# Sixteen gate columns of a gated DeltaNet: out of a product of their own, into a 272-wide group of the value projection

## The chip, the cores and the metric

The kernel runs on one core of a Trainium2 chip. The time is device microseconds for one execution of the whole program, and the figure given for a version is the median of its runs. Before the change the median is 1522.89 us of three runs (1521.16 to 1525.27).

In the listings PE is TensorE (matmuls and transposes; PEld is its weight load), ACT is ScalarE, DVE is VectorE, POOL is GpSimd, and SP is SyncE, which issues most DMAs. A tile is a buffer in the core's memory, with 128 partitions; a bank is one of the eight accumulator banks that PE writes.

## The reference, cut to what matters

The program computes one layer of a diffusion backbone: 1024 latent tokens and 256 context tokens of width 1024, together 1280 tokens, ten tiles of 128. What the change touches is the combined input projection and the gates made from 16 of its columns:

```python
h = concatenate([modulate(rms_norm(ctx)), modulate(rms_norm(x))])
p = h @ w_in
qkv_a, z, ab, rq, rk, rv, rg = split(p)      # 1536, 512, 16, 512, 512, 512, 512 columns
q, k, v = short_conv(qkv_a)                  # gated DeltaNet
a_f, a_b, b_f, b_b = split(ab, 4)            # 4 heads x 2 directions x 2 gates
g_f = -exp(A[0]) * softplus(a_f + dtb[0])    # g_b alike from a_b
o = gated_delta_rule(q, k, v, g_f, sigmoid(b_f))   # both directions
# retention on rq, rk, rv, then gates, output projection, SwiGLU, final RMSNorm
```

## The kernel before, in words

Everything is fp32. A large product is made of three matmuls: the operands are split into a high part (`hhi`, `whi`) and a remainder (`hlo`, `wlo`), and high times high, high times low and low times high are summed. `hhi` and `hlo` hold the normalized, modulated tokens with channels on partitions: 8 slices of 128 channels by 1280 tokens.

The stages that matter follow each other in the text like this.

- **Modulation** (L241 to L275). Tokens come in groups: two of 256 tokens, then one of 512 and one of 256 context tokens. Each tile is scaled on DVE (L259), transposed on PE (L266, tile `xtr`), and modulated. For the two later groups ACT writes `hhi` (L241) straight from the bank, DVE writes the scaled copy `hf` (L243), and DVE or POOL the remainder `hlo` (L244).
- **Value columns of retention** (`rv`), groups g = 0 and 1 of 256 columns each, by `token_major` (L334 to L350). The weights are loaded in two halves (`wraw`), split by ACT (`whi`, L287) and DVE (`wlo`, L288). For each of ten token tiles 24 matmuls (L343 to L345) fill a bank `tm` taken from the three `pa` banks, with a slice of `hhi` or `hlo` as the stationary 128x128 operand and 256 weight columns as the moving one. `fin_copy` on ACT copies the bank to `res` (L365), and a DMA that ACT issues stores it (L350). The latent tiles come first, the context tiles last. A bank can be filled again only when what was in it has been read.
- **The rest of adaLN** (`ada_rest`, L293): DVE sums (`acc`), then two short matmuls with a column of ones (`gr`, L309).
- **The gate columns** (L404 to L422). The 16 columns' weights `wabr` are loaded and split into 32 stationary columns (high and low beside each other). In three chunks of 256, 512 and 512 tokens, 48 matmuls `ab` (L413, L414) make a product with channels on partitions (32 x 1280). ACT copies it (L415), PE transposes it back in ten pieces (`abT`, L418), DVE copies and adds high and low (L420, L422). The result, `xa`, has tokens on partitions. What follows (softplus, `beta`, cumulative sums `G`, L423 to L456) reads `xa`.
- **The convolution blocks** (`conv_block`, L459 to L481): 12 blocks of 128 channels, channel-major, matmuls of 256 or 512 tokens (L468 to L470), two ACT evacuations, four taps on DVE, a SiLU on ACT. For keys and queries `kstat` (L488) transposes the result (`kt`). Between them stand `ada_rest` and more `token_major` groups (`rg` among them, from pool W2).
- **The solve** (`pre`, L557 to L600): for each token tile the product `kk` on PE (L557), decay matrices `e` on POOL (L575, L577), their product `ut` on DVE (L587), and then a triangular inverse that begins with a memset of `X` on POOL (L612).

The program is not issued in the order of the text. It is built with `schedule_with_timeline_sim=True`: a scheduler with a model of the engines orders each engine's instructions once, at build time. Each engine then works off its own row in that order, and waits at the head of the row where an operand isn't there yet or a buffer isn't free.

Of the kernel before, what the change touches and what calls it, by code (L numbers as in the profile page):

```python
# [8 lines left out]
F32 = mybir.dt.float32  # L9
F32R = mybir.dt.float32r  # L10
I32 = mybir.dt.int32
AF = mybir.ActivationFunctionType
ALU = mybir.AluOpType
# [4 lines left out]
P = 128  # L18
D = 1024
KT = D // P  # L20
NCTX = 256
NLAT = 1024
NTOK = NCTX + NLAT
TT = NTOK // P
# [13 lines left out]
def build(nc, tc, ap, dbg=None, stop=None, marks=None):  # L38
    root = ExitStack()
    V, S, G, T, SY = nc.vector, nc.scalar, nc.gpsimd, nc.tensor, nc.sync  # L40

    def pool(name, bufs=1, side=None, space=None):
        kw = {}
        if side is not None:
            kw["side"] = side
        if space is not None:
            kw["space"] = space
        if space is not DRAM:
            kw["reuse_waits"] = "tile"
        es = ExitStack()  # L50
        p = es.enter_context(tc.tile_pool(name=name, bufs=bufs, **kw))
        root.push(es)
        p_close[id(p)] = es
        return p
# [31 lines left out]
    def bank(tag, name):  # L86
        return PS["pool"].tile([P, 512], F32, tag=tag, name=name, bufs=PS["tags"][tag])

    def bank_a(name):
        return bank("pa", name)  # L90

    def bank_b(name):
        return bank("pb", name)
# [6 lines left out]
    def const(name, shape):  # L100
        t = C.tile(shape, F32, tag=name, name=name)
        S.dma_start(t, ap[name])
        return t
# [14 lines left out]
    def rsqrt_mean(pl, q, n, tag, num, x=None):  # L118


        s = pl.tile([P, n], F32, tag=tag + "s", name=tag + "s")
        y = pl.tile([P, n], F32, tag=tag + "y", name=tag + "y")
        u = pl.tile([P, n], F32, tag=tag + "u", name=tag + "u")
        if x is None:
            S.activation(s, q, AF.Sqrt, bias=epsb, scale=1.0 / num)
            x = pl.tile([P, n], F32, tag=tag + "x", name=tag + "x")
            V.tensor_scalar(x, q, -0.5 / num, -0.5 * EPS, ALU.mult, ALU.add)
            half = 1.0
        else:
            S.activation(s, x, AF.Sqrt)  # L130
            half = -0.5
        V.reciprocal(y, s)
        if n == 1 and half == 1.0:
            V.tensor_scalar(u, y, y, x, ALU.mult, ALU.mult)
        else:
            V.scalar_tensor_tensor(u, y, half, x, ALU.mult, ALU.mult)
            V.tensor_tensor(u, u, y, ALU.mult)
        V.scalar_tensor_tensor(y, u, 1.5, y, ALU.add, ALU.mult)
        return y
# [21 lines left out]
    try:  # L161

        cc = const("cc", [P, KT, 2])
        ident = const("ident", [P, P])
# [8 lines left out]
        hhi = LH.tile([P, KT, NTOK], F32R, tag="hhi", name="hhi")  # L173
        hlo = LH.tile([P, KT, NTOK], F32R, tag="hlo", name="hlo")
        W = pool("w", bufs=2)
# [18 lines left out]
        for k in range(KT):  # L194
            for i in range(2):
                w = P0.tile([P, 1024], F32, tag="adaw", name="adaw", bufs=7)
                last_ada = SY.dma_start(w, ap["ada_w"][k * P:(k + 1) * P, i * 1024:(i + 1) * 1024]).ins
                kw = {"skip_group_check": True} if k else {}
                if 2 * k + i in PLAIN:

                    for j in range(2):
                        T.matmul(psr[2 * i + j][:2, :], csl[:, k, :], w[:, j * 512:(j + 1) * 512],
                                 start=False, stop=(k == KT - 1), **kw)
                    continue
                whi = P0.tile([P, 1024], F32R, tag="adahi", name="adahi", bufs=2)
                wlo = P0.tile([P, 1024], F32R, tag="adalo", name="adalo", bufs=2)
                S.activation(whi, w, AF.Copy)
                V.tensor_tensor(wlo, w, whi.bitcast(F32), ALU.subtract)
                for j in range(2):
                    js = slice(j * 512, (j + 1) * 512)  # L210
                    o = psr[2 * i + j][:4, :]
# [8 lines left out]
        for i in range(2):  # L220
# [3 lines left out]
            for j in range(8):  # L224
                c0 = 4 * (8 * i + j)
# [20 lines left out]
        for gi, grp in enumerate(XGROUPS):  # L246
            n, t0 = len(grp), grp[0]
# [32 lines left out]
        R2 = pool("r2", bufs=2)  # L280
# [5 lines left out]
        def split(raw, hi, lo, e):  # L286
            S.activation(hi, raw, AF.Copy)  # L287
            e.tensor_tensor(lo, raw, hi.bitcast(F32), ALU.subtract)  # L288
# [30 lines left out]
                if c == 4:  # L319
                    V.scalar_tensor_tensor(o, o, 1.0, gffn[:, ks], ALU.add, ALU.mult)  # L320

        def weights(src, shape, e, pl, q=S, after=None):
            raw = pl.tile([P] + shape, F32, tag="wraw", name="wraw")
            if after is None:
                q.dma_start(raw, src)
            else:
                with tc.issue_after(after):
                    q.dma_start(raw, src)
            hi = pl.tile([P] + shape, F32R, tag="whi", name="whi")
            lo = pl.tile([P] + shape, F32R, tag="wlo", name="wlo")  # L330
            split(raw, hi, lo, e)
            return hi, lo

        def token_major(g, tiles, finish, store, pl, q=S, after=None):  # L334

            w = [weights(ap["wt"][g, :, 4 * kh:4 * kh + 4, :], [4, 256], V, pl, q, after) for kh in range(2)]
            c0 = (g % 2) * 256
            for t in tiles:
                tsl = slice(t * P, (t + 1) * P)
                o = bank_a("tm")[:, 0:256]  # L340
                for k in range(KT):
                    whi, wlo = w[k // 4]
                    T.matmul(o, hhi[:, k, tsl], whi[:, k % 4, :], start=(k == 0), stop=False)  # L343
                    T.matmul(o, hhi[:, k, tsl], wlo[:, k % 4, :], start=False, stop=False)  # L344
                    T.matmul(o, hlo[:, k, tsl], whi[:, k % 4, :], start=False, stop=(k == KT - 1))  # L345
                res = R1.tile([P, 256], F32, tag="res", name="res")
                finish(t, o, res)
                nm = GROUPS[g // 2]
                dst = zd[t - 2, :, c0:c0 + 256] if nm == "z" else rd[t, :, RD[nm], c0:c0 + 256]
                store.dma_start(dst, res)  # L350
# [20 lines left out]
        for g in range(2):  # L371
            token_major(g, ALL, fin_copy, S, W, SY, last_ada)
            ada_rest(2, g)
# [21 lines left out]
        AB = pool("ab", side="right")  # L395
# [4 lines left out]
        tri = AB.tile([P, 2, P], F32, tag="tri", name="tri")  # L400
        SY.dma_start(tri, ap["tri"])
        CHUNKS = [(0, 256), (256, 512), (768, 512)]

        wabr = AB.tile([P, KT, 16], F32, tag="wabr", name="wabr")  # L404
        SY.dma_start(wabr, ap["wab"])
        wab = AB.tile([P, KT, 32], F32R, tag="wab", name="wab")
        split(wabr, wab[:, :, 0:16], wab[:, :, 16:32], V)

        abc = AB.tile([32, NTOK], F32, tag="abc", name="abc")
        for c0, n in CHUNKS:  # L410
            ps = bank_b("ab")
            for k in range(KT):
                T.matmul(ps[:32, :n], wab[:, k, :], hhi[:, k, c0:c0 + n], start=(k == 0), stop=False)  # L413
                T.matmul(ps[:32, :n], wab[:, k, :], hlo[:, k, c0:c0 + n], start=False, stop=(k == KT - 1))  # L414
            S.activation(abc[:, c0:c0 + n], ps[:32, :n], AF.Copy)  # L415
        ps = bank_b("abT")
        for t in range(TT):
            T.transpose(ps[:, t * 32:(t + 1) * 32], abc[:, t * P:(t + 1) * P], ident[:32, :32])  # L418
        abT = AB.tile([P, TT, 32], F32, tag="abT", name="abT")
        V.tensor_copy(abT.rearrange("p t c -> p (t c)"), ps[:, :TT * 32])  # L420
        xa = AB.tile([P, TT, 16], F32, tag="xa", name="xa")
        V.tensor_tensor(xa, abT[:, :, 0:16], abT[:, :, 16:32], ALU.add)  # L422
        av = AB.tile([P, TT * 8], F32, tag="av", name="av")  # L423
        V.tensor_tensor(av.rearrange("p (t c) -> p t c", c=8), xa[:, :, 0:8],
                        bc(small["dtb"], [P, TT, 8], 1), ALU.add)
# [10 lines left out]
        ps = bank_b("G")  # L436
# [14 lines left out]
        ps = bank_b("GT")  # L451
# [86 lines left out]
        for g in (6, 7):  # L538
            token_major(g, LAT, fin_gate, S, W2, SY)
# [163 lines left out]
        for h in range(H):  # L703
            y = newy()
            conv_block(8 + h, y, False)
            for t0, n in ((0, 2), (2, 4), (6, 4)):
                ps = bank_b("vT")
# [22 lines left out]
        for g in (8, 9):  # L730
            token_major(g, LAT, fin_gate, S, W)
# [546 lines left out]
        w = {}  # L1278
# [52 lines left out]
        def finish(i, h):  # L1331
            l = 4 * h + i
            ssx = FO.tile([P, 1], F32, tag="ssx", name="ssx", bufs=4)
            V.tensor_tensor(ssx, sq[l][:, 0:1], sq[l][:, 1:2], ALU.add)
            rs = rsqrt_mean(FO, ssx, 1, "r%d" % i, D)
            G.tensor_tensor(xo[l][:, 0], xo[l][:, 0], fgr[:, 0], ALU.mult)
            for n in range(2):
                if n == 0:
                    S.activation(xo[l][:, 0], xo[l][:, 0], AF.Copy, scale=rs)
                else:  # L1340
                    V.scalar_tensor_tensor(xo[l][:, n], xo[l][:, n], rs, fgr[:, n], ALU.mult, ALU.mult)
                SY.dma_start(ap["out"][l * P:(l + 1) * P, n * 512:(n + 1) * 512], xo[l][:, n])
# [134 lines left out]
```

## Time and profile before

| | |
|---|---|
| median of three runs | 1522.89 us (1521.16 to 1525.27) |
| the profiled execution | 1518.69 us, its span 1516.9 us |
| mean granted TensorE clock | 0.977 |
| DVE / ACT / POOL busy, share of the span | 65% / 40% / 42% |
| modulation of the last two groups, with first matmuls of `rv` | about 50 to 80 us |
| matmuls of `rv`, `rk` and others, then `ab` | 80 to 125.4 us |
| convolution blocks and token-major groups | about 126 to 286.6 us |
| first `kk` that the solve waits for | 286.76 us |

Times in the listings are microseconds from the start of the span unless marked ns. In a group's row "x704" is the number of instructions. In a timeline row the first number is the start, the second the duration, and brackets at the end show idle time ahead of the instruction and what ended it. PE runs its matmuls overlapped, so the distance from one start to the next, not the duration of one, says what a matmul costs.

### The profile page before, as it was taken

The numbers are of one execution on the slowest core, as the hardware profiler recorded it, in microseconds if no ns is written. First come the engines' busy times: TensorE is split into PE (matmuls) and PEld (weight loads), VectorE is DVE, ScalarE is ACT, GpSimd is POOL, SyncE is SP. The second block draws the span as 40 slices with busy tenths as digits, with TensorE's granted clock in tenths as the row PEclk, the third lists the DMA queues.
The fourth block names the chain that finished last, engine by engine and source line by source line (L and its number), as shares of the span: only waits on it lengthen the run. The fifth ranks groups of instructions, "written<-read, shape, count | busy, mean of one in ns | idle before, by whom it ended". The sixth has DMA issues, their size and how long they took to land.

```text
span 1516.9 us, 24335 instructions
## 1 busy us (share of the span) xinstructions
PE 1441.7 (95%) x8973; PEld 1241.0 (82%) x8973; DVE 986.2 (65%) x1943; ACT 612.6 (40%) x1268; POOL 637.2 (42%) x589
## 2 busy tenths in 40 slices
PE   7899999987999999999689899999999999999997
PEld 1798887976989899999568778887888888888886
DVE  4955689379776634678847787655655555557477
ACT  4733454456451111325534443233333333354444
POOL 0300001476123233324306669889755553235321
PEclk9899999999989999999999999999999999999999
DMA  9374576587586464996843336676322232685962
GB/s 362 101 236 138 165 228 213 164 256 238 167 240 183 141 210 166 344 407 210 279 126 130 139 139 216 223 245 226 137 105 104 105 105 90 216 301 189 308 200 111
DMA packets 156487, 298.15 MB, mean 197 GB/s; under 512 B 43385, under 2 KB 75465, under 8 KB 150993
## 3 DMA queue, kind: packets, MB, share of 16 engines
q1 hardware_dynamic: 116624, 246.88, 48.3%
q10 hardware_dynamic: 36944, 41.08, 8.6%
q0 software_dynamic: 2800, 8.65, 1.6%
q8 instruction: 70, 1.15, 0.3%
q14 instruction: 49, 0.39, 0.1%
HBM read 206.60 MB, written 89.96 MB: 196 GB/s over the span
## 4 chain that ended last, share of the span: by engine, by line
PE 56%; POOL 8%; DVE 8%; DMA 7%; issue 4%; ACT 3%; ACTq 0%; SPq 0%; POOLq 0%; DVEq 0%
PE ffn L1168 6%; PE ffn L1166 6%; PE ffn L1167 6%; PE fo L1292 5%; PE fo L1294 5%; PE fo L1293 5%; PE tm L344 3%; PE tm L345 3%; PE tm L343 3%; DMA wd<-tw 2%; PE op L1026 1%; PE op L1027 1%; PE op L1025 1%; DMA gw<-grow_d 1%; POOL ws L1139 1%
## 5 line engine op out<-in xcount | busy, mean ns | idle before, releaser
L344 PE MATMUL tm<-wlo,hhi 128*128 128x256 f32 x704 | 205.3, 293 | 5.6 <-DVE wlo L288 5.6
L343 PE MATMUL tm<-whi,hhi 128*128 128x256 f32 x704 | 203.7, 293 | 5.9 <-ACT whi L287 2.4
L345 PE MATMUL tm<-whi,hlo 128*128 128x256 f32 x704 | 204.0, 292 | 0.0
L344 PEld LDWEIGHTS tm<-wlo,hhi 128*128 128x128 f32 x704 | 139.1, 198 | 8.4 <-DVE wlo L288 6.7
L343 PEld LDWEIGHTS tm<-whi,hhi 128*128 128x128 f32 x704 | 138.1, 198 | 8.0 <-ACT whi L287 3.0
L345 PEld LDWEIGHTS tm<-whi,hlo 128*128 128x128 f32 x704 | 138.6, 197 | 0.5 <-POOL hlo L244 0.2
L1166 PE MATMUL ffn<-t,whi 128*128 128x512 f32 x352 | 136.8, 390 | 1.4 <-ACT whi L287 1.4
L1168 PE MATMUL ffn<-t,wlo 128*128 128x512 f32 x352 | 136.9, 390 | 0.8 <-DVE wlo L288 0.8
L1167 PE MATMUL ffn<-t,whi 128*128 128x512 f32 x352 | 137.0, 389 | 0.0
L287 ACT ACTIVATE whi<-ws 128x512 fp32r<-128x512 f32 x88 | 55.6, 632 | 173.6 <-PE ffn L1167 122.3
L288 DVE TENSOR_TENSOR wlo<-ws,whi 128x512 fp32r<-128x512 f32 x88 | 95.1, 1082 | 46.9 <-ACT whi L287 46.7
L287 ACT ACTIVATE whi<-wraw 128x512 fp32r<-128x512 f32 (+1 forms) x98 | 75.2, 771 | 124.4 <-PE ffn L1167 81.6
L1293 PE MATMUL fo<-wlo,ahi 128*128 128x512 f32 x308 | 119.8, 389 | 0.0
L1292 PE MATMUL fo<-whi,ahi 128*128 128x512 f32 x308 | 119.3, 389 | 0.0
L1294 PE MATMUL fo<-whi,alo 128*128 128x512 f32 x308 | 119.0, 389 | 0.0
L288 DVE TENSOR_TENSOR wlo<-wraw,whi 128x512 fp32r<-128x512 f32 (+1 forms) x92 | 98.7, 1075 | 18.1 <-ACT whi L287 18.1
L1166 PE MATMUL ffn<-b,whi 128*128 128x512 f32 x264 | 103.9, 393 | 3.9 <-ACT whi L287 3.9
L1168 PE MATMUL ffn<-b,wlo 128*128 128x512 f32 x264 | 103.9, 393 | 2.1 <-DVE wlo L288 2.1
L1167 PE MATMUL ffn<-b,whi 128*128 128x512 f32 x264 | 103.4, 392 | 0.0
L468 PE MATMUL b<-hhi,whi 128*128 128x512 f32 (+1 forms) x256 | 94.2, 368 | 0.3 <-ACT y L472 0.3
L469 PE MATMUL b<-hlo,whi 128*128 128x512 f32 (+1 forms) x256 | 94.2, 368 | 0.0
L470 PE MATMUL b<-hhi,wlo 128*128 128x512 f32 (+1 forms) x256 | 93.9, 367 | 0.0
(431 smaller groups left out, 3586.4 us busy)
## 6 DMA issues: line engine op xcount, KB each, us to landing
adaw<-ada_w SPq DMA_DIRECT2D x48, 512.0 KB, 5.1
pk<-sd SPq DMA_DIRECT2D x16, 1536.0 KB, 7.9
wraw<-wfi SPq DMA_DIRECT2D x44, 512.0 KB, 3.7
ar<-ad SPq DMA_DIRECT2D x33, 512.0 KB, 4.6
w<-wfo SPq DMA_DIRECT2D x22, 512.0 KB, 5.1
wd<-tw SPq DMA_DIRECT2D x11, 1024.0 KB, 4.9
ad<-act SPq DMA_DIRECT2D x20, 512.0 KB, 2.9
raw<-wd SPq DMA_DIRECT2D x20, 512.0 KB, 6.1
```

What stands on the lines that cost most here:

```text
L287: S.activation(hi, raw, AF.Copy)
L288: e.tensor_tensor(lo, raw, hi.bitcast(F32), ALU.subtract)
L343: T.matmul(o, hhi[:, k, tsl], whi[:, k % 4, :], start=(k == 0), stop=False)
L344: T.matmul(o, hhi[:, k, tsl], wlo[:, k % 4, :], start=False, stop=False)
L345: T.matmul(o, hlo[:, k, tsl], whi[:, k % 4, :], start=False, stop=(k == KT - 1))
L468: T.matmul(o, whi[:, k, :], hh, start=(k == 0), stop=False)
L1166: T.matmul(o, whi[:, k, :], xhi(xn, slice(0, 4), k), start=(first and k == 0), stop=False, **kw)
L1167: T.matmul(o, whi[:, k, :], xlo(xn, slice(0, 4), k), start=False, stop=False, **kw)
L1168: T.matmul(o, wlo[:, k, :], xhi(xn, slice(0, 4), k), start=False, stop=(k == 3), **kw)
L1292: T.matmul(po[g][i], ahi[:, ts], whi, start=(j == 0 and not kw), stop=False, **kw)
L1293: T.matmul(po[g][i], ahi[:, ts], wlo, start=False, stop=False, **kw)
L1294: T.matmul(po[g][i], alo[:, ts], whi, start=False, stop=(j == FH - 1), **kw)
```

## The change

The 16 gate columns are appended to group g = 0 of the value columns. Its weight tiles are 272 columns wide, its 240 matmuls have a moving operand of 272 columns, and the bank holds 256 value columns and 16 gate columns with tokens on partitions. A small ACT instruction (new L354) copies the 16 columns of each token tile from the bank into `xa`, which now lives in pool R2. Lines L404 to L422 go: their load, split, 48 matmuls, three ACT copies, ten transposes and two DVE operations.

`weights` gets an argument `more`. The tiles of all users of pool W are made 272/256 as large; a group without the extra columns uses a slice of them, so that its pieces no longer lie end to end. The gate columns arrive by a second DMA for each half.

```diff
+        WIDE = 272
+        xa = R2.tile([P, TT, 16], F32, tag="xa", name="xa", bufs=1)
+
+        def weights(src, shape, e, pl, q=S, after=None, more=None):
+            m, n = shape
+            raw, hi, lo = (pl.tile([P, m, n * WIDE // 256 if pl is W else n], dt, tag=tag, name=tag)
+                           for dt, tag in ((F32, "wraw"), (F32R, "whi"), (F32R, "wlo")))
+            raw, hi, lo = (x if more is not None else x[:, :, :n] for x in (raw, hi, lo))
+            with tc.issue_after(after) if after is not None else nullcontext():
+                q.dma_start(raw[:, :, :n], src)
+                if more is not None:
+                    q.dma_start(raw[:, :, n:], more)
             split(raw, hi, lo, e)
             return hi, lo
...
-            w = [weights(ap["wt"][g, :, 4 * kh:4 * kh + 4, :], [4, 256], V, pl, q, after) for kh in range(2)]
+            w = [weights(ap["wt"][g, :, 4 * kh:4 * kh + 4, :], [4, 256], V, pl, q, after,
+                         ap["wab"][:, 4 * kh:4 * kh + 4, :] if g == 0 else None) for kh in range(2)]
...
-                o = bank_a("tm")[:, 0:256]
+                o = bank_a("tm")[:, 0:WIDE if g == 0 else 256]
...
-                finish(t, o, res)
+                finish(t, o[:, 0:256], res)
+                if g == 0:
+                    S.activation(xa[:, t, :], o[:, 256:WIDE], AF.Copy)
...
-        wabr = AB.tile([P, KT, 16], F32, tag="wabr", name="wabr")
-        SY.dma_start(wabr, ap["wab"])
-        wab = AB.tile([P, KT, 32], F32R, tag="wab", name="wab")
-        split(wabr, wab[:, :, 0:16], wab[:, :, 16:32], V)
-
-        abc = AB.tile([32, NTOK], F32, tag="abc", name="abc")
-        for c0, n in CHUNKS:
-            ps = bank_b("ab")
-            for k in range(KT):
-                T.matmul(ps[:32, :n], wab[:, k, :], hhi[:, k, c0:c0 + n], start=(k == 0), stop=False)
-                T.matmul(ps[:32, :n], wab[:, k, :], hlo[:, k, c0:c0 + n], start=False, stop=(k == KT - 1))
-            S.activation(abc[:, c0:c0 + n], ps[:32, :n], AF.Copy)
-        ps = bank_b("abT")
-        for t in range(TT):
-            T.transpose(ps[:, t * 32:(t + 1) * 32], abc[:, t * P:(t + 1) * P], ident[:32, :32])
-        abT = AB.tile([P, TT, 32], F32, tag="abT", name="abT")
-        V.tensor_copy(abT.rearrange("p t c -> p (t c)"), ps[:, :TT * 32])
-        xa = AB.tile([P, TT, 16], F32, tag="xa", name="xa")
-        V.tensor_tensor(xa, abT[:, :, 0:16], abT[:, :, 16:32], ALU.add)
```

The scheduler also orders the rows anew. Three places are shown. An entry names the line, the operation, output and inputs, the shape, and how many alike follow each other. Lines from L332 on have moved: the matmuls of `tm` are L343 to L345 before and L348 to L350 now, `res` is L365 and then L372, its store L350 and then L357, the blocks' matmuls L468 to L470 and then L455 to L457, `kk` L557 and then L544.

PE, in the modulation of the last two groups, before the change; `xtr` are the transposes of the token groups of 512 and 256:

```order
L266 MATMUL xtr<-ident,xt 128x128 x4
L343 MATMUL tm<-whi,hhi 128x256
L344 MATMUL tm<-wlo,hhi 128x256
L266 MATMUL xtr<-ident,xt 128x128 x4
L345 MATMUL tm<-whi,hlo 128x256
L343 MATMUL tm<-whi,hhi 128x256
L344 MATMUL tm<-wlo,hhi 128x256
```

PE at the same place with the change, behind the 72 matmuls of the first three token tiles:

```order
L348 MATMUL tm<-whi,hhi 128x272
L349 MATMUL tm<-wlo,hhi 128x272
L350 MATMUL tm<-whi,hlo 128x272
L266 MATMUL xtr<-ident,xt 128x128 x48
L348 MATMUL tm<-whi,hhi 128x272
L349 MATMUL tm<-wlo,hhi 128x272
L350 MATMUL tm<-whi,hlo 128x272
```

The 48 transposes of these two groups stood in many short runs with matmuls of `tm` between them, and now stand in one run. Of the 480 matmuls of groups 0 and 1, 195 stood ahead of the last of these transposes and 285 behind it; now 72 stand ahead and 408 behind.

ACT over the same stretch, before the change; `res` is the copy that empties a bank, and `hhi` the modulation:

```order
L125 ACTIVATE rx3s<-ms,epsb 128x2
L365 ACTIVATE res<-tm 128x256
L350 DMA rd<-res 128x256
L241 ACTIVATE hhi<-xtr,bmix,amix 128x512 x3
L365 ACTIVATE res<-tm 128x256
L241 ACTIVATE hhi<-xtr,bmix,amix 128x512
L350 DMA rd<-res 128x256
L241 ACTIVATE hhi<-xtr,bmix,amix 128x512 x4
L241 ACTIVATE hhi<-xtr,bmix,amix 128x256 x4
L365 ACTIVATE res<-tm 128x256 x2
```

ACT there with the change:

```order
L125 ACTIVATE rx3s<-ms,epsb 128x2
L372 ACTIVATE res<-tm 128x256
L357 DMA rd<-res 128x256
L241 ACTIVATE hhi<-xtr,bmix,amix 128x512 x8
L241 ACTIVATE hhi<-xtr,bmix,amix 128x256 x8
L354 ACTIVATE xa<-tm 128x16 x3
L414 ACT_TABLE_LOAD
L414 ACTIVATE nA<-alog 128x8
L372 ACTIVATE res<-tm 128x256
L354 ACTIVATE xa<-tm 128x16
```

The copies `xa` of the first three token tiles, which are the last readers of the three `pa` banks, stand behind all sixteen modulations `hhi`; copies `res` no longer stand among those.

PE near the end of the blocks, before the change, where the last run of `tm` matmuls (189 of them) ends and the first `kk` follow:

```order
L343 MATMUL tm<-whi,hhi 128x256
L344 MATMUL tm<-wlo,hhi 128x256
L345 MATMUL tm<-whi,hlo 128x256
L557 MATMUL kk<-kc 128x128 x8
L469 MATMUL b_3652<-hlo,whi 128x256
L470 MATMUL b_3652<-hhi,wlo 128x256
```

PE with the change, where that last run of 189 begins:

```order
L457 MATMUL b_3590<-hhi,wlo 128x256
L455 MATMUL b_3590<-hhi,whi 128x256
L544 MATMUL kk<-kc 128x128 x4
L348 MATMUL tm<-whi,hhi 128x256 x2
L456 MATMUL b_3590<-hlo,whi 128x256
L457 MATMUL b_3590<-hhi,wlo 128x256
```

Four `kk`, those of the first tile of the solve, have moved ahead of the last run of `tm`; the next eight still follow it. Between the gates and this place fewer `tm` matmuls stand between the blocks: ahead of the last transposes `kt` 158 stood there before, and 48 stand there now. On POOL, the memset of `X` stands at the same place in its row as before, and waits for PE in both.

More of the change, by code (lines that the diff above doesn't have):

```diff
@@ L320, in ada_rest @@
                     V.scalar_tensor_tensor(o, o, 1.0, gffn[:, ks], ALU.add, ALU.mult)
[L322 to L330, printed above, removed]
+        WIDE = 272
[9 more added lines that the diff above has]
+                    q.dma_start(raw[:, :, n:], more)
             split(raw, hi, lo, e)
```

## The prediction

> **What bounds the kernel now.** First the page's shares of busy time and, from its chain that ended last, the shares by engine:
>
> ```profile
> PE 1441.7 (95%) x8973; PEld 1241.0 (82%) x8973; DVE 986.2 (65%) x1943; ACT 612.6 (40%) x1268; POOL 637.2 (42%) x589
> PE 56%; POOL 8%; DVE 8%; DMA 7%; issue 4%; ACT 3%; ACTq 0%; SPq 0%; POOLq 0%; DVEq 0%
> ```
>
> PE is the bound on the whole. What the change is worth is read from the stages it touches, so next the windows up to the solve (start and end, length, busy time of PE, PEld, DVE, ACT and POOL with their counts, granted PE clock, DMA share, GB/s):
>
> ```profile
> 40.00:46.00 6.00, 4.08 (x14) 2.40 (x15) 6.00 (x13) 6.00 (x12) 3.15 (x4) 0.50 0.01 4
> 46.00:48.00 2.00, 2.00 (x10) 2.00 (x10) 2.00 (x5) 2.00 (x5) 0.54 (x1) 0.50 0.45 121
> 49.00:57.60 8.60, 8.60 (x74) 8.60 (x74) 8.25 (x20) 4.73 (x11) 3.10 (x4) 1.00 0.59 186
> 57.68:80.20 22.52, 20.49 (x170) 19.60 (x169) 17.59 (x31) 13.62 (x28) 8.69 (x8) 1.00 0.30 91
> 116.00:125.43 9.43, 9.43 (x49) 5.11 (x48) 6.21 (x8) 1.49 (x3) 2.89 (x1) 1.00 0.73 240
> 131.00:229.00 98.00, 98.00 (x581) 86.85 (x580) 67.46 (x118) 52.53 (x160) 5.01 (x2) 1.00 0.57 170
> 229.00:262.00 33.00, 31.65 (x156) 25.14 (x154) 29.93 (x45) 17.43 (x34) 5.33 (x2) 1.00 0.75 227
> ```
>
> From 49 us to the solve at 286.7 PE hardly stops. It idles 2.0 us while the last tokens are modulated (57.68 to 80.2), and 1.35 us in the row of 229 to 262. So whatever PE is spared there shortens the program, and each microsecond that it comes to idle there lengthens it.
>
> **The price of a matmul** comes from distances between starts. At 256 moving columns, the first and the last of 17 rows, 16 steps:
>
> ```profile
> 64.41 0.28 PE L343 MATMUL tm<-whi,hhi 128*128 128x256 f32 x1
> 66.32 0.28 PE L344 MATMUL tm<-wlo,hhi 128*128 128x256 f32 x1
> ```
>
> That is 1.91 us / 16 = 0.119 us each. At 512 columns, 9 rows, 8 steps:
>
> ```profile
> 152.09 0.39 PE L468 MATMUL b<-hhi,whi 128*128 128x512 f32 x1
> 153.91 0.39 PE L470 MATMUL b<-hhi,wlo 128*128 128x512 f32 x1
> ```
>
> 1.82 / 8 = 0.228 us. The difference over 256 columns gives 0.42 ns a column, so 16 more columns cost 6.8 ns a matmul.
>
> **What goes.** The gates' own matmuls and the transposes back:
>
> ```profile
> 116.04 0.30 PE L413 MATMUL ab<-hhi,wab 128*32 128x256 f32 x1
> 125.43 0.31 PE L418 MATMUL abT<-ident,abc 32*128 32x32 f32 x2
> 126.13 0.28 PE L468 MATMUL b<-hhi,whi 128*128 128x256 f32 x1
> 126.34 0.43 PE L418 MATMUL abT<-ident,abc 32*128 32x32 f32 x4
> 126.70 0.39 PE L469 MATMUL b<-hlo,whi 128*128 128x256 f32 x1
> ```
>
> `ab` takes PE from 116.04 to 125.43: **-9.4 us**, all of it on the path, since that window shows PE busy throughout. The ten `abT` come in a group of two and two of four. The group of four holds PE from 126.34 to 126.70; with 0.2 to 0.4 for each of the others I take **-1.2**. The ACT and DVE work that goes lies beside busy PE (DVE is busy 6.2 of 9.4 us in that window) and is worth nothing; nor do the softplus and `G` behind it hold anything up earlier.
>
> **What is added.** 240 matmuls become wider by 6.8 ns. The first 72 run ahead of 57.68, where PE must wait anyway for DVE to scale the last tokens. The other 168 cost 168 x 6.8 ns = **+1.1**. Ten copies `xa` on ACT cost some 0.21 us each, by the nearest small ACT row:
>
> ```profile
> L427 ACT ACTIVATE nA<-alog x1: 208/208/208, 88.0 to 88.0; 128x8 f32<-128x8 f32 x1
> ```
>
> Where PE doesn't wait for them they are hidden; ACT has 40% of the span.
>
> **What is moved: the first matmuls.** Here I expect the largest term. The new ACT row puts the first three `xa` behind all sixteen `hhi`. They are the last readers of the three `pa` banks, so no fourth token tile can begin until the modulation is over, and PE's row has the 48 transposes in one run ahead of the matmuls that wait. Before, 285 of the 480 matmuls were left after the last of these transposes, now 408. The other 123 cost 123 x 0.119 = **+14.7**, as PE stands idle or transposes while they could have run. Before, that point came here:
>
> ```profile
> 78.97 0.38 PE L266 MATMUL xtr<-ident,xt 128*128 128x128 f32 x2
> 79.10 0.36 PE L343 MATMUL tm<-whi,hhi 128*128 128x256 f32 x1
> ```
>
> Does the modulation end sooner without matmuls among it? Its pace, on DVE and ACT:
>
> ```profile
> 61.97 1.52 DVE L243 TENSOR_SCALAR hf<-xtr,amix,bmix 128x512 f32<-128x512 f32 x2
> 64.60 1.52 DVE L243 TENSOR_SCALAR hf<-xtr,amix,bmix 128x512 f32<-128x512 f32 x2
> 74.65 0.99 DVE L243 TENSOR_SCALAR hf<-xtr,amix,bmix 128x256 f32<-128x256 f32 x2 [0.35 <-ACT hhi L241]
> 76.21 0.99 DVE L243 TENSOR_SCALAR hf<-xtr,amix,bmix 128x256 f32<-128x256 f32 x2
> 79.92 0.57 ACT L241 ACTIVATE hhi<-xtr,bmix,amix 128x256 fp32r<-128x256 f32 x1 [0.41 <-ACT res L365]
> ```
>
> Two slices take 2.63 us at 512 tokens and 1.56 at 256. From 61.97, four pairs of each make 16.8 us: 78.7. ACT no longer has copies `res` among them, and ends its last `hhi` at about the same time instead of at 80.5; one `xa` of 0.21 us frees the first bank. With slack in the 512 pairs (2.2 us of DVE work in 2.63) I put the restart at 78.4, between 77 and 79.5: **-0.7** (-2.1 to +0.4).
>
> The transposes alone don't keep the clock up. In 40 to 46, with 14 PE groups, all transposes, the row above shows a granted clock of 0.50, and the matmuls after it run at that clock:
>
> ```profile
> 46.59 0.41 PE L343 MATMUL tm<-whi,hhi 128*128 128x256 f32 x1
> 47.45 0.41 PE L344 MATMUL tm<-wlo,hhi 128*128 128x256 f32 x1
> ```
>
> Four steps in 0.86 us, 0.215 each instead of 0.119. About 14 such steps lie between the first and the row of 49 us where the clock is full, 14 x 0.096 = **+1.3** if the clock falls again (0 to 1.7). [...]
>
> **Two smaller moves.** The 1.35 us of idle time in the row of 229 to 262 stand ahead of a matmul of `ada_rest`:
>
> ```profile
> 260.97 1.02 PE L309 MATMUL gr<-acc,ones 128*1 128x512 f32 x2 [1.35 <-DVE acc L304]
> ```
>
> In the new order other work surrounds it: **-1.35** (0 at worst). And four `kk` stand ahead of the last run of `tm`, so the first `ut` needn't follow its end:
>
> ```profile
> 286.76 0.90 PE kk L557 x8
> 287.75 2.01 DVE ut L587 x8
> 286.70 1.84 POOL L612 MEMSET X<- 128x1024 f32 x2 [11.55 <-PE tm L344]
> 289.04 3.49 POOL L575 TENSOR_SCALAR e<-gw,nG 128x128 f32<-128x128 f32 x8 [0.29 <-issue]
> 292.49 1.22 POOL L577 TENSOR_SCALAR_AFFINE_SELECT e<-e 128x512 f32<-128x512 f32 x2
> 294.09 0.87 DVE ut L587 x3
> ```
>
> But POOL still waits for the end of `tm` with the memset of `X`, ahead of the next `e` in its row. Memset 1.84, `e` 3.49 and the select stay in series; only the half microsecond between 288.54 and 289.04 can go: **-0.5** (0 to -0.8).
>
> **A term with no row: the filler between the blocks.** 110 fewer `tm` matmuls stand between the blocks ahead of the last `kt` (48 instead of 158), 13.1 us at 0.119. The same 98 us of the blocks come to have less PE work beside the same DVE and ACT work. DVE was busy 67.46 of 98.00; in 13.1 us less that would be 67.46/84.9 = 79%. The nearest row is 229 to 262: at 29.93/33.00 = 91% busy DVE, PE idled 1.35 us. So PE should mostly stay busy; I take **+1.0**. The bounds are 0 and 13.1, where the blocks keep their old pace whatever PE has to do.
>
> **Costed at nothing.** Slices of the wider tiles of pool W are split and read with gaps; no row shows such a split, and the nearest (`whi` and `wlo` of 128x1024 in one piece) are hidden beside PE, a group ahead. Were they slower by half, DVE would still have room in 131 to 229. Loads of W now land in small pieces, also a group ahead; only the first is met below.
>
> **The sum:** -9.4 - 1.2 + 1.1 + 14.7 - 0.7 + 1.3 - 1.35 - 0.5 + 1.0 = +4.95, rounded down to about +4.5, as the unpriced reordering has more to give than to take where PE idles in the solve. Against the profiled execution of 1518.69 us that is about 1523; this execution lies 4.2 us under the median of 1522.89, so the median would come to **1527 us**, 0.3% up.
>
> **The rivals.**
>
> *Work alone counts (8%).* If the `pa` banks are free sooner than the row of ACT says, the matmuls again fill the modulation. Then only -9.4 - 1.2 + 240 x 6.8 ns (1.6) = -9.0 remains: 1514. For it speaks that PE is the bound; against it, that ACT works its row in order and `xa` stands last.
>
> *The blocks lose their cover (17%), the slower side.* The place is between the gates and the last `kt`; the mechanism is that evacuations on ACT and the taps on DVE set the pace of a block once there is too little `tm` to put between. It decides when PE's share of a block falls below the DVE chain. Half of the 13.1 us instead of 1.0 gives about +10, 1533; all of it 1539. For it: DVE was at 91% in 229 to 262 already. Against it: three `y` buffers let blocks overlap, and 79% leaves room.
>
> *The solve begins early (15%).* If the memset of `X` and the second `e` find their buffers free before the last `tm`, the series of about 6.5 us (1.84 + 3.49 + 1.22) runs beside PE. Then +4.5 - 5 gives about 1522, no change. For it: `kk` has moved ahead. Against it: the memset stands where it did on POOL and waited 11.55 us for PE.
>
> *The first weights come late (7%).* The change adds two loads of the 16 columns in pieces of 64 bytes ahead of the first split. The nearest row of a load:
>
> ```profile
> wraw<-wt SPq DMA_DIRECT2D x4, 512.0 KB, 9.0
> ```
>
> If the small pieces delay the second half by a quarter of that, some 2.3 us, part of which the wait for the last tokens absorbs, the time is 1529 to 1530. [...]
>
> *Nothing named (8%)*: the changed order downstream of the gates, either way by 5 us or more.
>
> **How the numbers follow.** The forecast has 45%, its own range 1522 to 1531 by its bounds. Some 0.3% (4.6 us) is what a measurement here can tell from no change: 1518.3 to 1527.5. The forecast lies at the upper edge, so of its 45 I give 19 to slower, 25 to no change, 1 to faster. Slower: 19, 17 of the blocks, 4 of the late weights, 2 unnamed = 42%. Same: 25, 13 of the early solve, 3 of the late weights, 2 unnamed = 43%. Faster: 1, 8 of work alone, 2 of the early solve, 4 unnamed = 15%. The range 1516 to 1535 leaves out the first rival and the worst of the second.
>
> **What would show it.** In the new profile: a window around 58 to 78 with only transposes on PE and the clock at 0.50 at its end; `xa` L354 three times behind the last `hhi`; the first 272-wide `tm` of the fourth tile at about 78, ended by ACT; no `ab`; PE busy again to a `kk` some 5 us later than 286.76. Wrong would be: `tm` among the transposes; PE idle by microseconds inside the blocks, released by ACT or DVE; `ut` well ahead of the end of `tm`; the first `tm` later than 46.

## The result, and the profile after

The changed kernel takes 1535.92 us (median of five runs, 1532.61 to 1542.21) against 1522.89 (five runs, 1520.17 to 1525.27). The ratio is 1.0096, with a 95% interval of 1.0067 to 1.0124: 13 us slower. The forecast was 1527, with a range up to 1535.

Its page, the line on busy time:

```profile
PE 1444.7 (94%) x8915; PEld 1242.7 (81%) x8915; DVE 978.8 (64%) x1940; ACT 606.9 (40%) x1268; POOL 637.1 (42%) x589
```

58 PE instructions fewer, and yet PE is busy 3.0 us longer, in a span (1530.8 us) that is 13.9 us longer: what was lost is waiting, and time at a lower clock (0.965 over the span, 0.977 before). The windows of the changed kernel over the same stretches as before, and the one behind the modulation:

```profile
57.68:80.20 22.52, 13.00 (x63) 9.23 (x61) 19.42 (x33) 13.57 (x27) 7.26 (x7) 0.61 0.25 85
80.20:100.00 19.80, 19.80 (x147) 19.80 (x148) 8.94 (x13) 5.71 (x15) 0.73 (x1) 0.92 0.67 219
131.00:229.00 98.00, 98.00 (x539) 83.59 (x538) 72.64 (x110) 51.25 (x158) 10.05 (x4) 1.00 0.67 202
229.00:262.00 33.00, 33.00 (x186) 27.38 (x185) 28.46 (x48) 13.90 (x30) 2.40 (x1) 1.00 0.73 227
```

While the last tokens are modulated (57.68 to 80.2), PE was busy 20.49 of 22.52 us and now 13.00, at a granted clock of 0.61 instead of 1.00; it begins the next stretch at a lowered clock (0.92 over 19.80 us). The blocks (131 to 262) keep PE busy throughout. So the row of 229 to 262 has lost its 1.35 us of idle time, and no new wait has come in for the missing filler.

The PE timeline of the changed kernel over that stretch, some rows:

```profile
65.35 1.97 PE L266 MATMUL xtr<-ident,xt 128*128 128x128 f32 x8 [4.64 <-DVE hf L243]
...
78.64 0.69 PE L266 MATMUL xtr<-ident,xt 128*128 128x128 f32 x2 [0.40 <-DVE hf L243]
80.06 0.59 PE L348 MATMUL tm<-whi,hhi 128*128 128x272 f32 x1 [0.73 <-ACT xa L354]
```

Only transposes, in runs that wait for DVE, and then the first matmul of the fourth token tile, which waits for the copy `xa` (L354). That is the pile-up as foretold. To follow it through the program I use two marks: the first memset of `X` on POOL, which waits for the last `tm` ahead of the solve, and the first `vT` (transposes of the value blocks, behind the first stretch of the solve). In a tile's row the times after the durations are the first and the last start. Before, and below it the changed kernel:

```profile
L612 POOL MEMSET X<- x3: 952/952/953, 286.7 to 399.7; 128x1024 f32 x3
L709 PE MATMUL vT<-ident,y x40: 271/273/474, 366.0 to 405.1; 128*128 128x128 f32 x40
```

```profile
L599 POOL MEMSET X<- x3: 951/951/952, 294.0 to 410.4; 128x1024 f32 x3
L696 PE MATMUL vT<-ident,y x40: 270/273/476, 375.9 to 413.6; 128*128 128x128 f32 x40
```

The solve begins 7.3 us later (294.0 against 286.7 us). But at the end of the span the changed kernel is 13.9 late. About half of the loss lies **behind** the start of the solve, where no line of the kernel was changed.

### The profile page after: what moved, and what is told of

Same layout as the page of the kernel before. It is cut to its first block, busy times and chain, and to the rows that moved or that the text cites. A ratio compares the mean times of both kernels' runs of the same rounds, so it can differ in the third digit from the quotient of the medians.

```text
span 1530.8 us, 24239 instructions
## 1 busy us (share of the span) xinstructions
PE 1444.7 (94%) x8915; PEld 1242.7 (81%) x8915; DVE 978.8 (64%) x1940; ACT 606.9 (40%) x1268; POOL 637.1 (42%) x589
## 4 chain that ended last, share of the span: by engine, by line
PE 72%; DVE 7%; POOL 7%; DMA 6%; ACT 4%; issue 3%; ACTq 0%; SPq 0%; POOLq 0%; DVEq 0%
PE ffn L1155 7%; PE ffn L1154 7%; PE ffn L1153 7%; PE fo L1279 5%; PE fo L1281 5%; PE fo L1280 5%; PE tm L349 4%; PE tm L350 4%; PE tm L348 4%; PE b L455 3%; PE b L456 3%; PE b L457 3%; DMA wd<-tw 2%; PE op L1014 1%; PE op L1013 1%
## 5 line engine op out<-in xcount | busy, mean ns | idle before, releaser
L348 PE MATMUL tm<-whi,hhi 128*128 128x256 f32 (+1 forms) x704 | 204.2, 293 | 8.1 <-ACT whi L287 4.1
L349 PE MATMUL tm<-wlo,hhi 128*128 128x256 f32 (+1 forms) x704 | 206.3, 294 | 5.5 <-DVE wlo L288 5.5
L350 PE MATMUL tm<-whi,hlo 128*128 128x256 f32 (+1 forms) x704 | 205.9, 293 | 0.0
L348 PEld LDWEIGHTS tm<-whi,hhi 128*128 128x128 f32 x704 | 138.4, 198 | 11.0 <-ACT whi L287 5.2
L350 PEld LDWEIGHTS tm<-whi,hlo 128*128 128x128 f32 x704 | 139.5, 198 | 2.5 <-issue 1.7
L288 DVE TENSOR_TENSOR wlo<-wraw,whi 128x512 fp32r<-128x512 f32 (+2 forms) x92 | 104.5, 1137 | 49.7 <-ACT whi L287 49.6
L287 ACT ACTIVATE whi<-wraw 128x512 fp32r<-128x512 f32 (+2 forms) x98 | 75.3, 772 | 133.3 <-PE ffn L1154 90.2
L288 DVE TENSOR_TENSOR wlo<-ws,whi 128x512 fp32r<-128x512 f32 x88 | 90.8, 1032 | 37.4 <-ACT whi L287 36.9
L465 DVE SCALAR_TENSOR_TENSOR y<-u,cw,y 128x1022 f32<-128x1022 f32 (+3 forms) x80 | 80.3, 1015 | 30.1 <-ACT y L459 29.7
L455 PE MATMUL b<-hhi,whi 128*128 128x512 f32 (+1 forms) x256 | 95.9, 375 | 0.2 <-ACT y L459 0.2
```

The lines of the kernel that those rows point to most:

```text
L455: T.matmul(o, whi[:, k, :], hh, start=(k == 0), stop=False)
```

## The experiments

Two theories on the first half: the *place* of `xa` (it lies in pool R2, which the text opens right after it closes the modulation's pool P0; that R2 takes over memory of P0, and a tile there waits until what lay in it is done with, is inferred from the text and the rows, as no run shows the addresses), against the *pieces* (wide tiles, 64-byte loads). A third, the *order downstream*, is about the second half.

**xa elsewhere.**

```diff
-        xa = R2.tile([P, TT, 16], F32, tag="xa", name="xa", bufs=1)
+        xa = C.tile([P, TT, 16], F32, tag="xa", name="xa", bufs=1)
```

> The changed kernel with the gate columns xa in the pool of constants instead of pool R2, nothing else. Theory (place): xa in R2 lies where pool P0 of the modulation lay, so its copies, and with them the three pa banks, wait for the end of the modulation; in C they don't. In PE's row 197 matmuls of tm then stand ahead of the last transpose instead of 72, so 125 x 0.119 = 14.9 us and 1.3 of slow clock come back: about 1520 against 1536, and with nothing lost downstream 1514. Rival (pieces): the 272-wide tiles and 64-byte pieces cost the time; then xa's place is worth at most 3 us, 1533 or more. Rival (order downstream): the front gains the 15 us but the solve and scans keep their new order's loss of some 8 us: 1521 or a little more.

Measured: 1515.86 us against 1522.09 of before in the same series, ratio 0.9955 (0.993 to 0.9981). Another pool's name turns a loss of 0.96% into a gain of 0.45%. The window of this kernel's modulation, and its memset:

```profile
57.68:80.20 22.52, 21.52 (x172) 20.72 (x172) 16.30 (x29) 13.63 (x32) 7.83 (x7) 1.00 0.29 87
L599 POOL MEMSET X<- x3: 952/953/954, 277.5 to 394.4; 128x1024 f32 x3
```

The window holds 172 PE instructions again (63 in the changed kernel), at full clock, and the solve begins 16.5 us earlier than in the changed kernel. The time lies between what *place* alone gave (1514 with nothing lost downstream, 1520 by its first bound) and is far from *pieces*. The third theory, the order downstream, had put it at 1521 or more, and missed it by 5 us.

**The R2 copy alone.** The kernel before, and only this:

```diff
+        xw = R2.tile([P, TT, 16], F32, tag="xw", name="xw", bufs=1)
...
+                if g == 0:
+                    S.activation(xw[:, t, :], o[:, 0:16], AF.Copy)
```

> The kernel before, with ten added ACT copies of 16 columns of each token tile of group 0 into a tile of pool R2, which nothing reads; the gates' own product stays, tiles stay 256 wide. Theory (place): 72 matmuls of tm ahead of the last transpose instead of 195, so +14.7 and +1.3 for the slow clock: about 1539. Rival (pieces): nothing changes, 1523. Rival (order downstream): +10 to +16 at the front, then what the scheduler makes of it.

Measured: 1543.71 us, ratio 1.0144 (1.0106 to 1.0183). Ten copies that nothing reads cost 21.6 us, 5 more than expected. The trace puts the memset at 302.5, 15.8 later than before. So the pile-up needs neither the wide tiles nor the missing product. (This trace is the fastest of six runs, 1537.31; the median is 6 us above it.)

**Wide tiles alone.** The kernel before with the new `weights`, without `more`.

> The kernel before, with the weight tiles of pool W 272/256 as large and sliced, so that splits and loads go in pieces; no gate columns in them. Theory (place): 1523, within 4. Rival (pieces): +5 or more, with PE waiting for whi and wlo.

Measured: 1527.24 us, ratio 1.0022 (0.9993 to 1.005). Unclear: between the two. Its trace has the memset at 285.6, no later than before, so up to there the wide tiles cost nothing; a few us behind it remain possible by the median.

**Without the gates' product.** The kernel before, with lines L404 to L421 gone and `V.memset(xa, 0.5)` for L422.

> The kernel before without the gates' load, split, 48 matmuls, transposes, copies and addition; xa is filled with 0.5 instead, so the gates are wrong. It prices what the change removes. Theory (place): -9.4 - 1.2 = -10.6, about 1512. Rival (order downstream): the new order (48 matmuls of tm instead of 116 ahead of the last kt, the first kk ahead of the last run of tm, as in the changed kernel) gives back some 8 us of it: 1519 or more. Pieces says nothing here.

Measured: 1512.42 us, ratio 0.993 (0.9908 to 0.9952), so -9.7: near the price of the product. But the memset comes at 274.7, 12.0 earlier than before. 2.3 us of it by the median, 9.3 by the one trace, are given back behind it. By the median the theory's 1512 held, and the rival's 1519 or more did not; the trace, 3.6 us slower than the median, says the opposite.

**The same two kernels again**, for one more trace each.

> The kernel before, traced once more, to see how far two executions of one program differ by stage. Theory (order downstream): up to the memset of X on POOL (286.7) and from there to the end (1230.2) both within 1.5 us of the first trace. Rival (executions differ): the part behind X differs by 3 us or more, so that much of the 6.6 us which the changed kernel lost there by its one trace isn't the change's.

> The changed kernel, traced once more. In its first trace the memset of X came at 294.0 and the end 1236.8 us behind it, 6.6 more than in the first trace of before. Theory (order downstream): again 294 and 1236 to 1238. Rival (executions differ): X at 294 again, what is behind it 3 us or more off.

Measured: spans of 1519.6 and 1529.7, with memsets at 286.7 (the kernel before) and 292.8 (the changed one). Up to the solve, two executions of a program agree to 1.2 us. Behind it the kernel before takes 1230.2 and 1232.9 us, the changed one 1236.8 and 1236.9. Neither expectation was met in full: 2.7 us are the executions', and over 5 look like the kernels'. Does taking the product out bring the loss? The table sets the single traces (span less memset) beside the medians of each version's runs (less the 1.8 us outside the span, and less the memset of its trace, or the mean of two):

| version | memset to end, by the traces | by the median |
|---|---|---|
| with the gates' product: before | 1230.2, 1232.9 | 1234.4 |
| R2 copy alone | 1232.7 | 1239.4 |
| wide tiles | 1229.3 | 1239.8 |
| without it: changed | 1236.8, 1236.9 | 1240.7 |
| xa elsewhere | 1237.5 | 1236.6 |
| no product | 1239.5 | 1235.9 |
| one copy (below) | 1239.4 | 1237.6 |

By the traces the two groups don't overlap, and their means are 6.7 us apart. But a trace is one execution, and 29 executions of the kernel before lie between 1511.31 and 1530.94 us, the fastest at a granted clock of 0.981, the slowest at 0.970. By the medians the groups overlap. So that every version without the product is slower behind the memset isn't shown. It is shown for the changed kernel (6.3 us by the medians, over 5 by the traces); for the other three without the product the medians leave 1.5 to 3.2 us, which their intervals don't tell from nothing. What does divide all nine traces is the first stretch, from the memset to the first `vT`: 75.7 to 79.3 us in the four with the product, 81.3 to 82.2 in the five without.

**One copy of 272 columns:** in the changed kernel ACT empties the whole bank into a wide `res`, and POOL takes `xa` from there.

> The changed kernel, but ACT empties each bank of group 0 with one copy of 272 columns, and POOL takes the 16 gate columns to xa (still in R2) from that copy. The banks no longer hang on xa, only the copies' buffers do (two of them): 120 matmuls of tm stand ahead of the last transpose, between 72 (changed) and 197 (xa elsewhere). Theory (place): 48 x 0.119 = 5.7 us earlier than the changed kernel at the solve, X at 288 to 289, time 1528 to 1530. Rival (it is the separate small copies on ACT that cost): as fast as with xa elsewhere, 1516.

Measured: 1527.82 us, ratio 1.0023 (1.0 to 1.0046), memset at 288.4. With 72, 120 and 197 matmuls ahead of the last transpose the memset stands at 293.4 (mean of two), 288.4 and 277.5: 0.10 us for each matmul of the first step and 0.14 of the second, around the 0.119 of the forecast. So the loss follows the number of matmuls that the held banks keep back; that the small copies as such cost it is out.

**Late memset.** `xa` in C, and

```diff
-            G.memset(X, 0.0)
-            G.memset(X[:, 0::33], 1.0)
+            with tc.issue_after(last_e[0]):
+                G.memset(X, 0.0)
+                G.memset(X[:, 0::33], 1.0)
```

where `last_e[0]` is the last select on POOL.

> xa in the pool of constants, and the memset of X on POOL put behind the last e of its batch in the text's order of issue, so that the e of the second tile no longer stands behind a memset that waits for the last tm. Theory (the solve's start is bound by this series): the wait of kk for ut (4.4 us) goes and the solve starts 4 to 7 us earlier: 1510 to 1512 against 1515.9. Rival (PE or DVE bounds the solve's start anyway, or a later wait takes its place): within 2 us of xa elsewhere.

Measured: 1519.86 us, ratio 0.9974 (0.995 to 0.9998). The stretch gains what the theory said (the first `vT` at 353.2 against 359.7), and nothing of it is left in the time, which is 4.0 us above *xa elsewhere* by the medians: nearer to the rival, though outside its 2 us as well. (Its trace is a run of 1514.21.)

**Splits off POOL.** What is different in the stretch from the memset to the first `vT`? The one row of `wlo` on POOL there, before and then in the changed kernel:

```profile
329.76 3.32 POOL L288 TENSOR_TENSOR wlo<-wraw,whi 128x1024 fp32r<-128x1024 f32 x1
```

```profile
333.79 2.36 POOL L288 TENSOR_TENSOR wlo<-wraw,whi 128x1024 fp32r<-128x1024 f32 x1 [4.37 <-ACT whi L287]
```

A value block's weight split stands on POOL between the decay matrices `e`. Before, its `whi` was ready; in the new order POOL waits 4.37 us for ACT, with `e` queued behind it. The five traces without the product in the table have this wait; of the four with it none waits more than 0.2 us. (The late memset, also without the product, has no such wait in its order, so its 6.5 us may come from that too.) To test it, in the kernel with `xa` in C:

```diff
-            whi, wlo = weights(ap["wg"][b], [KT, P], G if b % 2 else V, W)
+            whi, wlo = weights(ap["wg"][b], [KT, P], G if b % 2 and b < 8 else V, W)
```

> xa in the pool of constants, and the weights of the four convolution blocks of the values split on DVE only, so that no split stands on POOL between the e of the solve. In five traces without the gates' product POOL waits 4.4 us there for ACT (whi), splits for 2.4 us, and the stretch from the memset of X to the first vT takes 81.3 to 82.2 us; in four traces with it POOL doesn't wait, and it takes 75.7 to 79.3. Theory (POOL's wait in the solve is what the new order costs): the stretch falls by 4 to 6 us to 76 to 78, and the time from 1515.9 to 1510 to 1512. Rival (e and ut set the pace whether or not POOL waits there; the loss lies in their order): the stretch stays at 80 to 82 and the time within 2 us of xa elsewhere.

And the same in the kernel before:

> The kernel before with the same edit, as a control. Theory (POOL's wait in the solve): POOL has no wait to lose here, only a split of 3.3 us: the stretch from X to the first vT loses 0 to 3 us, the time 0 to 3. Rival (the split itself, not the wait, is the price): the stretch falls by as much as in the version without the gates' product, 4 to 6 us.

Measured: the stretch falls from 82.2 to 78.4 us (277.4 to 355.8) without the product, and in the kernel before to 77.6 (287.3 to 364.9; it was 79.3 and 77.8). That is 3.8, and 0.2 to 1.7. So with the split off POOL most of the stretch's loss goes where POOL had the wait, and little where it had none. But each `e` became shorter too (593 ns on average instead of 622), so the wait, the split and the slower `e` aren't told apart.

The times are 1537.38 (ratio 1.0093, 1.0066 to 1.0119) and 1540.86 (1.0085, 1.0052 to 1.0118): the expectation of 1510 to 1512 failed by 25 us, and that of at most 3 us less in the control by 17 the other way. The scheduler made another order from there on: from the memset to the first matmul of the output projection (`op`) the first takes 507.5 us instead of 477.9, the second 495.4 instead of 473.1 and 476.5. What both traces show there is a lowered clock. From the first `vT` to `op` it is 0.89 over 429.10 us without the product, against 0.96 over 395.70 in *xa elsewhere*; in the control it is 0.91 over 417.80, against 0.96 and 0.94 in the two traces of before. The largest piece lies in the triangular inverse; the windows of *xa elsewhere* and then of the same with the splits off POOL:

```profile
439.00:479.00 40.00, 40.00 (x537) 38.33 (x537) 28.53 (x74) 7.38 (x13) 12.12 (x22) 0.96 0.56 155
436.00:476.00 40.00, 40.00 (x458) 38.21 (x455) 21.25 (x54) 6.42 (x11) 4.83 (x9) 0.62 0.34 96
```

PE is busy throughout in both, and 0.34 x 40.00 = 13.6 us of full clock are lost. Among the small products of the inverse (32x32 and 64x64) stand 185 matmuls `tm` in the first window and 93 in the second. In the kernel before and its control it is alike: 164 `tm` at a clock of 0.91 (446 to 486), 100 at 0.63 (445 to 485). In both pairs the window with fewer `tm` has the lower clock; whether the one brings the other no run tests. Nor does the low clock come in every execution: of the control's ten, four took 1525.75 to 1528.62 us at a clock of 0.974 to 0.979 over the span, and six 1540.45 to 1544.77 at 0.963 to 0.969, its trace among these. An edit that shortens its own stretch thus tells little of the whole time.

## Why the prediction was wrong

**The front was right in its main steps.** `xa` stands behind the last `hhi`; the transposes stand alone; the clock fell (0.61 over 57.68 to 80.2); the restart waits for `xa`. The restart came at 80.06 in the first trace and 78.78 in the second, for 78.4: the load of the context tokens, for which ACT waits ahead of this modulation, was issued at 53.27 and 52.15 instead of 50.46, and with it came the whole modulation. One reading was loose: of the 14 PE instructions of the row of 40 to 46, twelve are transposes and two are `tm`. The changed kernel shows the same with transposes alone: 0.50 over 65 to 80. But PE also idled in both stretches, busy 4.08 of 6.00 us there and 9.83 of 15.00 here, so the two don't tell whether the clock fell for the transposes or for the idle time. For the slow clock the forecast had +1.3 us, from the rows, and up to 1.7: no run shows that bound, and the changed kernel lost 1.6 us (last section).

The sum for the pile-up was 14.7 + 1.3 - 0.7 = 15.3; it measured 15.8 (R2 copy alone, against before) and 16.5 or 15.3 (the changed kernel's two traces, against xa elsewhere). The removal was -9.4 - 1.2 - 1.35 = -11.95 at the solve; the kernel without the product shows -12.0. The widening was +1.1; xa elsewhere against no product shows +2.8 at the memset, which has the ten copies and the wide tiles in it too. The filler's +1.0 was nothing: PE was busy 98.00 of 98.00 and 33.00 of 33.00, with DVE at 74% in the first of the two windows.

Up to the solve the forecast's terms come to +5.45; measured were +7.3 and +6.1.

**The cause was read one step short.** The prediction took the late `xa` from ACT's row and didn't ask why the scheduler had put it there. The runs answer it: with `xa` in another pool the copies come early again, and an unread copy in R2 alone brings the loss. The reason for it, that R2 takes over the modulation's memory, is inferred. It would not have changed the forecast, but it would have shown that the loss isn't a price of the idea.

**The first weights** came later, but not by the rival of 7%. The first `wlo` matmul starts at 48.15 in the first trace of the changed kernel and at 46.97 in the second, for 46.00 and 45.81 in the two of before. Neither split waits for a load there: ACT's first `whi` stood ahead of a sum of squares (`junk`) and now stands behind it, and `wlo` stands later in DVE's row. That the pieces of 64 bytes delay anything isn't shown; the rival's quarter of a load's 9.0 us was an estimate of the author's.

**What failed is the step behind the memset:** "rounded down to about +4.5, as the unpriced reordering has more to give than to take where PE idles in the solve". The solve's onset, from the memset to the second tile's `ut`, stands in these rows, before (its memset is at 286.70) and then changed:

```profile
293.82 2.16 DVE L587 SCALAR_TENSOR_TENSOR ut<-kk,ab,e 128x128 f32<-128x128 f32 x8 [1.88 <-ACT e L579]
```

```profile
293.95 1.84 POOL L599 MEMSET X<- 128x1024 f32 x2 [19.56 <-PE tm L349]
300.77 2.16 DVE L574 SCALAR_TENSOR_TENSOR ut<-kk,ab,e 128x128 f32<-128x128 f32 x8 [1.52 <-ACT e L566]
```

That is 6.8 us instead of 7.1, a gain of 0.3 where 0.5 was forecast. For the rest the forecast had another gain, the 0.45 of the rounding, with no row behind it. Instead the changed kernel lost 5.3 us behind the memset by the two traces of each kernel, and 6.3 by the medians: the sign of the term was wrong. *Nothing named* had 8% for "either way by 5 us or more", and this is what came, on the slow side. 3.1 of the 5.3 us lie between the memset and the first `vT`. There POOL waits 4.4 us for `whi` between the `e` of the solve, and each `e` takes longer (last section); with the split off POOL most of the loss in that stretch went, and with it a part of the slower `e`. The prediction showed `e` on POOL in the series that starts the solve, and yet didn't look for what else the new order put into POOL's row there. The other 2 to 3 us, behind the first `vT`, stay open. The trace of a version lies up to 10.5 us under its median (wide tiles) or 3.6 over it (no product), so what single traces show behind the memset is as rough as that.

So +6.7 at the front and +5.3 behind it make the 12.0 between the mean traces (1530.25 and 1518.25), and the medians differ by 13.0.

**The rivals.** *Work alone counts* fell, but would have been nearly the right account for another place of `xa`: 1515.9 with that edit, against 1514 forecast for it. *The blocks lose their cover* fell: no idle time. *The solve begins early* fell: the memset still waited for the last `tm`, 19.6 us by the profile.

## What to carry to other kernels

Before a new small tile goes into a pool, ask when a tile of that pool can first be written. Ten copies into R2 that nothing reads cost 21.6 us, as they are the last readers of accumulator banks and came only behind the modulation; with `xa` in a pool that is open from the start, the changed kernel was 20 us faster. Put a tile that empties a bank into such a pool.

Where a scheduler orders the program, price an edit by marks, not by the end: the part up to the next common mark came out as summed to about 2 us, while the part behind it moved by 5 to 30 us, with the order and from one execution to the next. Give reordering a term of its own, with both signs. Look in the new order at what stands in the row of the engine that starts each later stage, and set medians of many runs beside single traces.

## What the runs showed of the hardware that was not expected

With 48 transposes among 63 PE instructions, and PE busy in 13.00 of 22.52 us, the granted clock was 0.61 over 57.68 to 80.2, and 0.92 over the next 19.80 us: 0.08 x 19.80 = 1.6 us of full clock were lost, for 1.3 forecast from the rows. PE was busy throughout from the restart at 80.06 to 100, and the clock was 0.51 over 80.06 to 83.30 and 1.00 over 83.30 to 100.

The same `e` of 128x128 on POOL became slower. From the memset to the first `vT`, before and then changed (count, busy us, mean ns):

```profile
L575 POOL TENSOR_SCALAR e<-gw,nG 128x128 f32<-128x128 f32 x56 | 29.6, 548 | 12.4 <-DMA gw<-grow_d 6.7 <-DVE sp L589 3.9 <-DVE ut L587 1.4
```

```profile
L562 POOL TENSOR_SCALAR e<-gw,nG 128x128 f32<-128x128 f32 x58 | 35.1, 622 | 11.4 <-DVE ut L574 5.1 <-DVE sp L576 2.2 <-DMA gw<-grow_d 2.2
```

74 ns more on each of some 57 make 4 us, beside POOL's wait for `whi`. In the other three traces with the product `e` takes 510, 510 and 559 ns, in the other four without it 611 to 622; even two executions of the kernel before differ (548 and 510). No run here shows the reason.

A PE that is busy all the time can have a lowered clock: 0.62 over 40.00 us of 40.00 busy, with small products and 93 `tm` matmuls among them, where 0.96 was granted with 185.
